# Eight tiles of u fetched at the first dense tile, later Gelus, and three rows moved from v to u, in a decoder trunk with expert retrieval

## The chip, the cores and the metric

The kernel runs on one core of one Trainium2 chip. The metric is the device time of one execution in microseconds (us), lower is better.

## The reference

Two pre-norm residual layers over 256 positions of width 1024. The first layer's mixer is block-sparse attention beside chunkwise retention, the second's a gated short convolution. Each layer ends in an expert mixer (PEER), which is what the change touches:

```python
def peer(xn, w_q, sub_keys, u, v):
    ...
    q = (t @ w_q).reshape(n_tok, PEER_HEADS, 2, PEER_DKEY // 2)
    sc = jnp.einsum('thpd,hpnd->thpn', q, sub_keys).astype(jnp.float32)
    s1, i1 = lax.top_k(sc[:, :, 0], PEER_TOPK)
    s2, i2 = lax.top_k(sc[:, :, 1], PEER_TOPK)
    ...
    top_s, pos = lax.top_k(cand, PEER_TOPK)
    eidx = jnp.take_along_axis(cidx, pos, axis=-1)
    gate = jax.nn.softmax(top_s, axis=-1).astype(xn.dtype)
    ...
        hid = jax.nn.gelu(jnp.einsum('td,thkd->thk', tc, u[ec]), approximate=False)
        return jnp.einsum('thk,thkd->td', gc * hid, v[ec])
```

Per token, 8 heads choose 16 of 16,384 experts each; the token's product with the chosen rows of u goes through a Gelu and a gate, and weighs the chosen rows of v.

## The kernel before

The 256 tokens of the expert mixer are split. For 96 of them (`TG`) the 128 chosen rows of u, and later of v, are fetched from memory one expert slot at a time: one indirect DMA of POOL's queue brings 128 rows of 1024 floats (a "row" below, 192 per layer: 96 of u, then 96 of v). For the other 160 (`TD`) all experts are computed densely: 128 tiles of u, each [128, 1024], are multiplied with the tokens, and Gelu and a gate matrix G, built from one-hot matrices, give HG; then 128 tiles of v are multiplied with HG.

So a layer's mixer has these stages:

- Query tiles: 16 tiles of `wq`, each split in a high and a low part (pools `hi` and `lo`, 3 buffers each), with the scores against the keys (`ko`) one tile behind. VectorE runs the top-16 searches from a list of pieces (`pump`).
- u: the loop over 128 dense tiles `dense_u(i)`. Each uses one of four PSUM tiles. ScalarE's Gelu (L1400, L1402) and, once G has begun, VectorE's product (L1403) read it. Up to about tile 54 VectorE still works off the pump; then the indices are turned (`idx_tr`), and from about tile 61 G is built, 40 groups, two per three tiles.
- v: the loop over 128 tiles of v, 95 of them split in two parts by ScalarE (L1378) and VectorE (L1385).

Dense tiles come through a ring of 8 raw buffers (`Stream`): a load on SP's queue is told when its buffer's tile eight before has been told to be used, and waits on the queue until TensorE is done with it. SP's queue is in order: whatever stands behind a waiting load waits too. 22 of the 128 u tiles (`PRE`, tile number to buffer number) don't go through the ring: `fetch(i)` loads them into memory that is idle at that time. Fourteen go into the area of HG and the accumulators of the rows and are fetched during the query tiles (`early`). The other eight go into buffers that come free only after the last query tile (`early_u`, in this order: tile 58 into a `lo` buffer and `one`, 64 and 76 into `hi` buffers, 82 into `Xb`, 94 into a `hi` buffer, 106 into two `lo` buffers, 23 and 43 into the keys' `ko`). They are told one per dense tile, i = 1 to 8, each behind that tile's ring load.

The rows run beside all that (`Gather`): six buffers; `consume` tells VectorE's work on the next row (L985 for u, L1002 for v) and `issue` tells POOL to fetch the next one into the buffer. `ga.rate` is the number of rows consumed per dense tile: 0.6 for the first 8, 0.9 in tiles 8 to 45, 0.6 until G begins, then what brings the count to `UPTO[l]` rows (112 in layer 0, 110 in layer 1) at tile 117; the rest of the 192 is spread over v. After each quarter of 32 rows of u, `later` holds two pieces that are told when a later row is consumed: ScalarE's Gelu of the sums of those 32 rows (L991), 2 rows after the quarter's last, and VectorE's product with the gates (L992), 4 rows after it.

Of the kernel before, what the change touches and what calls it, by code (L numbers as in the profile page):

```python
# [14 lines left out]
AF = mybir.ActivationFunctionType  # L15
OP = mybir.AluOpType
# [12 lines left out]
NK = 128  # L29
# [13 lines left out]
GT = 4  # L43
UNIT = 2.0 ** 15
SCR = 11 * D
UPTO = (112, 110)
SPL = [i for i in range(NK) if i % 2 or i % 4 == 0 and i > 0]
CODE = 64.0
WHOLE = 1.5 * 2.0 ** 23
# [3 lines left out]
CALM = 11  # L53
# [141 lines left out]
def trunk_kernel(ctx, tc, x, small, cst, mcst, ew_in, ew_out, ow_in, ow_out, wq, keys, pu, pv, pun, gains, out):  # L195
    nc = tc.nc
    v = nc.vector
    act = nc.scalar
# [51 lines left out]
    def nm(s):  # L250
        uid[0] += 1
        return f"{s}{uid[0]}"
# [414 lines left out]
    def new_ko(dtype=F32):  # L667

        n = NPAIR * NK * (2 if dtype is F16 else 1)
        xv["ko"] = pers.tile([P, n], dtype, tag="ko", name=nm("ko"))  # L670
        return xv["ko"]
# [266 lines left out]
    class Gather:  # L938
# [39 lines left out]
        def consume(self):  # L978
            s_ = self.c
            r = self.row(s_)  # L980
            j = s_ % STEPS
            q = j // SUB
            w = self.hid[:, j:j + 1]
            if s_ < STEPS:
                v.scalar_tensor_tensor(r, r, 1.0, XG[:, q % 2, :], op0=OP.mult, op1=OP.mult, accum_out=w)  # L985
                if s_ == SUB - 1:
                    gp.dma_start(XG[TG:, 0, :], XG[2 * SUB:TG, 0, :])
                if j % SUB == SUB - 1:
                    w = self.hid[:, q * SUB:(q + 1) * SUB]
                    g = IG[:, 1, q * SUB:(q + 1) * SUB]  # L990
                    self.later[s_ + 2] = lambda: act.activation(w, w, AF.Gelu)  # L991
                    self.later[s_ + 4] = lambda: v.tensor_tensor(w, w, g, OP.mult)  # L992
            elif j % SUB == 0:
                so_far = self.acc[q - 1] if q else h[:, 0, :]
                v.scalar_tensor_tensor(self.acc[q][:TG], r[:TG], w[:TG], so_far[:TG], op0=OP.mult, op1=OP.add)
                v.tensor_scalar(self.acc[q][TG:], r[TG:], w[TG:], None, op0=OP.mult)
                if q:
                    self.part(q - 1)
                if q == 2:
                    self.later[s_ + 8] = self.fold  # L1000
            else:
                v.scalar_tensor_tensor(self.acc[q], r, w, self.acc[q], op0=OP.mult, op1=OP.add)  # L1002
            self.later.pop(s_, lambda: None)()
            self.c += 1
# [17 lines left out]
    def peer(l, before, norm):  # L1022
        with tc.tile_pool(name=nm("hg"), bufs=1) as hp:
# [36 lines left out]
            ga = Gather(hp)  # L1060
# [8 lines left out]
            def fetch(i):  # L1069

                k = PRE[i]
                if k < 11:
                    t = [flat[:, k * D:(k + 1) * D]]
                elif k < 14:
                    t = [ga.acc[k - 11]]
                elif 14 < k < 18:
                    t = [st.hi_pool.tile([P, D], F32R, tag="hi", name=nm("uhi")).bitcast(F32)]
                elif k > 19:  # L1080
                    if k == 20:
                        there["ko"] = new_ko().rearrange("p (a d) -> p a d", a=2)
                    t = [there["ko"][:, k - 20, :]]
                elif k == 18:
                    t = [Xb.rearrange("p k s -> p (k s)").bitcast(F32)]
                else:
                    n = 1 if k == 14 else 2
                    t = [st.lo_pool.tile([P, D], BF16, tag="lo", name=nm("ulo")).bitcast(F32) for _ in range(n)]
                    t += [one] * (2 - n)
                n = D // len(t)  # L1090
                for j, p in enumerate(t):
                    nc.sync.dma_start(p, pu[l, i][:, j * n:(j + 1) * n])
                there[i] = [p[:, c:c + P] for p in t for c in range(0, n, P)]
# [3 lines left out]
            early_u = [i for i in sorted(PRE) if PRE[i] >= 14]  # L1097
            early_u = early_u[2:] + early_u[:2]
# [184 lines left out]
            def after_first():  # L1283

                scores(NPAIR - 1)
                pump.add((1.35, stage1(0, NPAIR - 1, NPAIR)))
                chain(0, 1)
                pump.add((0.3, lambda: gates(0)), (0.6, lambda: places(1)))
                pump.add(*[(2.7, stage1(1, f, f + 2)) for f in range(HH * 2, NPAIR, 2)])
                pump.add((0.0, lambda: gates_exp(0)))  # L1290
                chain(1, 0)
                pump.add((0.6, lambda: gates_norm(0)), (0.3, shares))
                chain(1, 1)
                pump.add((0.3, lambda: gates(1)), (3.0, None), (0.0, lambda: gates_exp(1)), (3.0, None),
                         (0.6, lambda: gates_norm(1)), (3.0, None), (3.0, None), (0.5, idx_tr), (3.0, None))
# [3 lines left out]
            def onehots(g):  # L1299

                oh = xv["gate"][:, :6 * GT * P].rearrange("p (n j t i) -> p n j t i", n=3, j=2, i=P)[:, g % 3]
                hi = xv["gate"][:, 6 * GT * P:].rearrange("p (n t i) -> p n t i", n=2, i=P)[:, g % 2]
                v.tensor_tensor(oh, iota[:, None, None, :].to_broadcast([P, 2, GT, P]),  # L1303
                                idxT[:, :2, g * GT:(g + 1) * GT][:, :, :, None].to_broadcast([P, 2, GT, P]),
                                OP.is_equal)
                ohs[g] = oh[:, 0], hi, oh[:, 1]
# [32 lines left out]
            gst = {"g": -1, "credit": 0.0, "rate": 0.0}  # L1339

            def slot(n):

                g = gst["g"]
                shared()
                if g < 0 or g >= NG:
                    return
                gst["credit"] += gst["rate"]
                if gst["credit"] < 1.0:
                    return
                gst["credit"] -= 1.0  # L1350
                ps = g_mm(g)
                if g + 3 < NG:
                    onehots(g + 3)
                if g + 2 < NG:
                    todo.append(g + 2)
                g_put(g, ps, n)
                gst["g"] = g + 1

            def dense_u(i):
                if i in PRE:  # L1360
                    w = there.pop(i)
                else:
                    t = st.next()
                    w = [t[:, k * P:(k + 1) * P] for k in range(ND)]
                ps = acc_tile(i % 4, nm("hid")) if i % 4 < 2 else hid_tile(nm("hid"))
                for k in range(ND):
                    pe.matmul(ps[:, :TD], w[k], XF[:, k, :], start=k == 0, stop=k == ND - 1)  # L1367
                    if k == ND // 2 - 1:
                        slot(i)
                return ps  # L1370
# [17 lines left out]
            for i in range(NK):  # L1388
                ps = dense_u(i)
                if i == 0:  # L1390
                    after_first()
                elif early_u:
                    fetch(early_u.pop(0))
                if i == NK - 1:
                    gst["rate"] = 1.0
                    while gst["g"] < NG:
                        slot(i)
                T = max(gst["g"], 0) * GT
                if T < TD:
                    act.activation(HG[:, i, T:], ps[:, T:TD], AF.Gelu)  # L1400
                if T > 0:
                    act.activation(ps[:, :T], ps[:, :T], AF.Gelu)  # L1402
                    v.tensor_tensor(HG[:, i, :T], ps[:, :T], HG[:, i, :T], OP.mult)  # L1403
                slot(i + 1)
                if gst["g"] < 0:
                    if i == first_late - 2:
                        pump.flush()
                    if pump.q:
                        pump.run(1.4)
                    else:  # L1410
                        gst["g"] = 0
                        gst["rate"] = NG / (2.0 * (NK - 10 - i))
                        gst["credit"] = -0.6
                        xv["gate"] = new_ko(F16)
                        for g in range(3):
                            onehots(g)
                        todo += [0, 1]
                        shared()
                        shared()
                ga.rate = (0.9 if 8 <= i < 46 else 0.6) if gst["g"] < 0 else (UPTO[l] - ga.c) / (NK - CALM - i) if i < NK - CALM else 0.6  # L1420
                if i < NK - QUIET:
                    ga.step()
                elif i in (NK - QUIET, NK - QUIET + 2):
                    weight_parts(i - NK + QUIET + 1)
# [41 lines left out]
            for i in range(NK):  # L1466
                j = i + AHEAD
# [22 lines left out]
                w = st.next()  # L1490
# [85 lines left out]
```

## Time and profile before

| | us |
|---|---|
| median of 3 runs | 1489.36 (1488.99 to 1492.16) |
| the profiled execution | 1490.58 |
| its span, first to last instruction | 1488.8 |
| u of layer 0, about | 182 to 490 |
| v of layer 0, about | 490 to 751 |
| u of layer 1, about | 907 to 1212 |
| v of layer 1, about | 1212 to 1472 |

Busy shares of the span: TensorE 97%, VectorE 84%, ScalarE 51%, GpSimd 50%; mean granted TensorE clock 0.997. The DMA engines moved 532.80 MB, 358 GB/s over the span.

In the views, PE is TensorE's matmul and PEld its weight load, DVE VectorE, ACT ScalarE, POOL GpSimd, SPq the queue on which SP issues DMAs. A line of the chain is start, duration, and what; of the timeline start, duration, engine, line and operation; of the waits who waited for whom, the total in us, how often, and the longest.

### The profile page before, as it was taken

The page shows a single profiled execution, that of the slowest core. Times are in us where ns is not written, and L with a number is a line of the kernel's source. Part 1 is how long each engine was busy: PE and PEld are TensorE (multiplying, and loading weights), DVE is VectorE, ACT ScalarE, POOL GpSimd, SP SyncE. Part 2 cuts the span into 40 slices and gives each one's busy share as a digit, 9 for nine tenths or more (in the row PEclk, how much of TensorE's full clock was granted, in tenths as well). Part 3 has the DMA queues.
Part 4 walks back from the last instruction along what each step waited for, and adds up shares of the span by engine and source line. Part 5 has one row for each costly group of instructions (what it writes and reads, how often), then busy time and mean ns, then how long its engine had stood idle before and what let it go on. Part 6 is the DMA issues. An engine that isn't in the chain of part 4 may idle for free.

```text
span 1488.8 us, 30108 instructions
## 1 busy us (share of the span) xinstructions
PE 1438.1 (97%) x11184; PEld 1334.8 (90%) x11184; DVE 1246.5 (84%) x2467; ACT 761.3 (51%) x1825; POOL 744.9 (50%) x513
## 2 busy tenths in 40 slices
PE   9999999999999999999989999999999999999997
PEld 5667999999999998889889799999999999988886
DVE  5637999879999788888876589996899978888888
ACT  6556511258875454445564463212888745454544
POOL 6754545546667243345335374453566643443532
PEclk9999999999999999999999999999999999999999
DMA  8545899999999999999966478999999999999995
GB/s 322 199 145 203 311 378 409 395 409 408 405 402 396 394 400 405 406 394 404 409 242 230 169 277 326 407 408 396 408 405 401 399 397 407 399 408 409 398 406 228
DMA packets 147618, 532.80 MB, mean 358 GB/s; under 512 B 16976, under 2 KB 17360, under 8 KB 147472
## 3 DMA queue, kind: packets, MB, share of 16 engines
q1 hardware_dynamic: 72288, 258.43, 44.9%
q0 software_dynamic: 56608, 204.81, 35.1%
q10 hardware_dynamic: 18576, 67.64, 11.5%
q8 instruction: 88, 1.44, 0.4%
q14 instruction: 58, 0.48, 0.1%
HBM read 528.40 MB, written 1.05 MB: 356 GB/s over the span
## 4 chain that ended last, share of the span: by engine, by line
PE 54%; issue 17%; POOL 11%; DMA 9%; DVE 7%; ACT 2%; POOLq 0%; DVEq 0%; ACTq 0%; SPq 0%
PE hid L1367 30%; POOL rows L975 7%; PE hid L261 5%; DMA raw<-pu 4%; DMA raw<-pv 3%; POOL grow L975 3%; PE hid L267 2%; PE G L1327 2%; DMA rows<-pv,ig 2%; PE ea L295 2%; PE vo L1501 2%; PE ea L294 2%; PE ea L293 2%; DVE gacc L1002 1%; PE vo L1497 1%
## 5 line engine op out<-in xcount | busy, mean ns | idle before, releaser
L1367 PE MATMUL hid<-xf,raw 128*128 128x160 f32 x3392 | 487.4, 301 | 7.3 <-DMA raw<-pu 4.6
L1367 PEld LDWEIGHTS hid<-xf,raw 128*128 128x128 f32 x3392 | 467.1, 191 | 10.5 <-issue 5.6
L1378 ACT CAST vhi<-raw 128x1024 fp32r<-128x1024 f32 x190 | 198.5, 1046 | 266.1 <-DMA raw<-pv 218.9
L975 POOL DMA_INDIRECT rows<-pv,ig x128 | 192.5, 1504 | 209.2 <-DVE gacc L1002 180.0
L1385 DVE TENSOR_TENSOR vlo<-raw,vhi 128x1024 bf16<-128x1024 f32 x190 | 231.9, 1223 | 77.4 <-ACT vhi L1378 69.1
L1501 PE MATMUL vo<-ko,vhi 128*128 128x320 f32 x1520 | 270.5, 320 | 24.5 <-DVE ko L1460 23.5
L1501 PEld LDWEIGHTS vo<-ko,vhi 128*128 128x128 f32 x1520 | 224.3, 188 | 33.8 <-DVE ko L1460 32.5
L975 POOL DMA_INDIRECT rows<-pun,ig x128 | 170.7, 1334 | 136.0 <-DVE rows L985 63.2
L151 POOL TENSOR_TENSOR lo<-raw,hi 128x1024 bf16<-128x1024 f32 x70 | 167.9, 2408 | 85.7 <-ACT hi L149 82.8
L985 DVE SCALAR_TENSOR_TENSOR rows<-rows,xg 128x1024 f32<-128x1024 f32 x128 | 155.5, 1220 | 22.5 <-DMA rows<-pun,ig 22.4
L1400 ACT ACTIVATE hg<-hid 128x160 f32<-128x160 f32 (+14 forms) x240 | 62.7, 265 | 199.1 <-PE hid L1367 199.0
L1002 DVE SCALAR_TENSOR_TENSOR gacc<-rows,ghid,gacc 128x1024 f32<-128x1024 f32 x124 | 158.8, 1281 | 4.7 <-DMA rows<-pv,ig 3.9
L975 POOL DMA_INDIRECT grow<-pv,ig x64 | 99.7, 1558 | 122.8 <-DVE gacc L1002 110.9
L1497 PE MATMUL vo<-hg,raw 128*128 128x160 f32 x1056 | 157.3, 302 | 1.0 <-DVE hg L1403 1.0
L1497 PEld LDWEIGHTS vo<-hg,raw 128*128 128x128 f32 x1056 | 145.5, 190 | 1.4 <-DVE hg L1403 1.4
L1503 PE MATMUL vo<-hb,vlo 128*128 128x160 bf16 x1520 | 138.1, 234 | 2.1 <-DVE vlo L1385 2.1
L1317 ACT ACTIVATE ko<-ko,idxT 128x128 f16<-128x128 f16 x320 | 101.8, 390 | 51.1 <-DVE ko L1303 50.9
L1503 PEld LDWEIGHTS <-vlo 128*128 128x128 bf16 x1520 | 100.5, 98 | 22.1 <-DVE vlo L1385 3.1
L975 POOL DMA_INDIRECT grow<-pun,ig x64 | 81.3, 1270 | 77.6 <-DVE grow L985 43.3
L149 ACT CAST hi<-raw 128x1024 fp32r<-128x1024 f32 x100 | 102.8, 1046 | 30.0 <-PE hid L261 18.5
L261 PE MATMUL hid<-x,hi 128*128 128x256 f32 x800 | 107.4, 287 | 0.2 <-DVE cg L912 0.2
L1320 ACT ACTIVATE ko<-ko,idxT 128x128 f16<-128x128 f16 x320 | 101.1, 388 | 0.0
(251 smaller groups left out, 2097.2 us busy)
## 6 DMA issues: line engine op xcount, KB each, us to landing
raw<-pu SPq DMA_DIRECT2D x212, 512.0 KB, 7.9
raw<-pv SPq DMA_DIRECT2D x128, 512.0 KB, 8.9
raw<-pv ACTq DMA_DIRECT2D x128, 512.0 KB, 8.0
raw<-wq SPq DMA_DIRECT2D x32, 512.0 KB, 3.9
raw<-ew_in SPq DMA_DIRECT2D x28, 512.0 KB, 4.5
raw<-ow_in SPq DMA_DIRECT2D x24, 512.0 KB, 5.3
hg<-pu SPq DMA_DIRECT2D x22, 512.0 KB, 5.1
raw<-ew_out SPq DMA_DIRECT2D x8, 512.0 KB, 3.1
```

Of the source, the lines that this page charges most:

```text
L149: self.nc.scalar.copy(hi, t)
L151: eng.tensor_tensor(lo, t, hi.bitcast(F32), OP.subtract)
L261: pe.matmul(ps[:, :S], hi[:, k * P:(k + 1) * P], A2[:, k, s_, :], start=k == 0 and s_ == 0, stop=False)
L975: gp.indirect_dma_start(self.row(s_), None, table, bass.IndirectOffsetOnAxis(IG[:, 0, s_ % STEPS:s_ % STEPS + 1].bitcast(U32), 0))
L985: v.scalar_tensor_tensor(r, r, 1.0, XG[:, q % 2, :], op0=OP.mult, op1=OP.mult, accum_out=w)
L1002: v.scalar_tensor_tensor(self.acc[q], r, w, self.acc[q], op0=OP.mult, op1=OP.add)
L1367: pe.matmul(ps[:, :TD], w[k], XF[:, k, :], start=k == 0, stop=k == ND - 1)
L1378: act.copy(whi[j], raw)
L1385: v.tensor_tensor(wlo[j], raw, whi[j].bitcast(F32), OP.subtract)
L1497: pe.matmul(vo[b][:, :TD], w[:, b * P:(b + 1) * P], HG[:, i, :], stop=False, **m)
L1501: pe.matmul(vo[b][:, :2 * TD], hi[:, b * P:(b + 1) * P], hs, stop=i == NK - 1, **m)
L1503: pe.matmul(vo[b][:, :TD], lo[:, b * P:(b + 1) * P], hb, stop=i == NK - 1, **m)
```

## The change

Three edits in the expert mixer, the same in both layers. The eight fetches of `early_u` are all told at i = 0, behind the last scores, instead of one each at i = 1 to 8. The Gelu of the fetched sums is told 12 rows after its quarter's last row instead of 2, and the product with the gates 16 rows after instead of 4. And three more rows are consumed in u: `UPTO` is (115, 113), with a rate of 0.93 instead of 0.9 in tiles 8 to 45; the rate over v is worked out from what is left, so v has three rows fewer.

```diff
-UPTO = (112, 110)
+UPTO = (115, 113)
...
-                    self.later[s_ + 2] = lambda: act.activation(w, w, AF.Gelu)
-                    self.later[s_ + 4] = lambda: v.tensor_tensor(w, w, g, OP.mult)
+                    self.later[s_ + 12] = lambda: act.activation(w, w, AF.Gelu)
+                    self.later[s_ + 16] = lambda: v.tensor_tensor(w, w, g, OP.mult)
...
                 if i == 0:
                     after_first()
-                elif early_u:
-                    fetch(early_u.pop(0))
+                    for j in early_u:
+                        fetch(j)
...
-                ga.rate = (0.9 if 8 <= i < 46 else 0.6) if gst["g"] < 0 else (UPTO[l] - ga.c) / (NK - CALM - i) if i < NK - CALM else 0.6
+                ga.rate = (0.93 if 8 <= i < 46 else 0.6) if gst["g"] < 0 else (UPTO[l] - ga.c) / (NK - CALM - i) if i < NK - CALM else 0.6
```

## The prediction

> **What bounds the kernel now.** I read the page's rates first, then the chain of waits around the start of the dense u tiles, the SP queue's timeline there, the same stretches by windows, and the waits.
>
> ```profile
> span 1488.8 us, 30108 instructions
> GB/s 322 199 145 203 311 378 409 395 409 408 405 402 396 394 400 405 406 394 404 409 242 230 169 277 326 407 408 396 408 405 401 399 397 407 399 408 409 398 406 228
> raw<-pu SPq DMA_DIRECT2D x212, 512.0 KB, 7.9
> ```
>
> A slice is 37.2 us. From the sixth to the twentieth slice (layer 0) and again from the twenty-sixth to the thirty-ninth (layer 1) the DMA engines stand at 378 to 409 GB/s and never rise above 409: a ceiling. Those are the two experts' mixers. By stage (PE, PEld, DVE, ACT, POOL busy, clock, DMA share, GB/s), with the last hole before each plateau first, then u, u, v, v:
>
> ```profile
> 182.00:190.00 8.00, 8.00 (x63) 8.00 (x61) 7.55 (x24) 3.75 (x9) 2.52 (x4) 1.00 0.46 172
> 907.00:918.00 11.00, 11.00 (x84) 11.00 (x83) 10.31 (x39) 4.06 (x10) 4.92 (x7) 1.00 0.60 216
> 190.00:490.00 300.00, 295.99 (x2329) 292.83 (x2328) 271.68 (x660) 153.84 (x561) 169.54 (x126) 0.99 1.02 404
> 918.00:1212.00 294.00, 290.68 (x2302) 287.53 (x2301) 266.16 (x642) 151.34 (x556) 162.12 (x121) 1.00 1.02 404
> 490.00:751.00 261.00, 247.38 (x2058) 232.54 (x2057) 222.43 (x204) 129.06 (x164) 106.47 (x72) 1.00 1.02 402
> 1212.00:1470.00 258.00, 245.04 (x2040) 230.65 (x2039) 221.92 (x204) 128.55 (x163) 108.78 (x75) 1.00 1.02 403
> ```
>
> So in u TensorE and the DMA engines are both full (296 of 300 us; 404 GB/s), and in v the DMA engines alone. A tile or a fetched row is 512 KB, 524,288 B / 404 GB/s = 1.30 us of all DMA engines: my price for everything moved. The v stage ends with rows on the chain, and ScalarE waits for raw tiles of v all through it:
>
> ```profile
> 736.49 14.85 DMA rows<-pv,ig
> 1462.03 9.59 DMA rows<-pv,ig
> ```
>
> ```profile
> ACT vhi L1378 <- DMA raw<-pv: 218.9, 102, 4.9
> ACT hg L1209 <- DVE hg L1205: 6.7, 2, 4.1
> ACT ghid L991 <- DVE grow L985: 6.2, 2, 3.8
> ```
>
> **The eight fetches.** Today one is issued per tile, each behind the raw load of its tile on SP's queue (layer 0, then layer 1):
>
> ```profile
> 178.84 0.56 SPq L1092 DMA_DIRECT2D one<-pu  x1
> 187.53 0.33 SPq L134 DMA_DIRECT2D raw<-pu  x1
> 187.90 0.43 SPq L1092 DMA_DIRECT2D uhi<-pu  x1
> ...
> 202.28 0.33 SPq L1092 DMA_DIRECT2D ko<-pu  x1
> ```
>
> ```profile
> 904.28 0.43 SPq L1092 DMA_DIRECT2D one<-pu  x1
> 912.23 0.33 SPq L134 DMA_DIRECT2D raw<-pu  x1
> ...
> 928.21 0.33 SPq L1092 DMA_DIRECT2D ko<-pu  x1
> ```
>
> The first (ulo and one) is out by 178.84. The raw at 187.53 waits until TensorE has done with tile 1, and the other seven stand behind it and its followers: SP idles 8.7 us (8.0 in layer 1) while the DMA engines drain. The buffers are free far sooner:
>
> ```profile
> 182.25 0.45 PE sc L1117 x4
> 182.70 2.18 PE hid L1367 x16
> 184.87 0.44 PE sc L1117 x4
> 185.32 19.56 PE hid L1367 x144
> 204.88 19.64 DMA raw<-pu
> 224.52 0.14 issue
> 224.65 84.50 PE hid L1367 x608
> ```
>
> The last query tile's matmuls, which read the last hi, lo and Xb, end at 182.25; the keys (ko) are read last by the four at 184.87, done at 185.3. With all eight told at i = 0 they are ahead of that raw on the queue, and SP (some 0.4 us an issue) has two uhi out near 179.5, xb, uhi and two ulo near 182.5 to 184, both ko by 186. Seven tiles are 9.1 us of DMA work. The hole is worth 8 x (1 - 172/404) = 4.6 us in layer 0 and 11 x (1 - 216/404) = 5.1 us in layer 1; I take 0.3 us off each, since xb and the two ko come free only inside the hole: **4.3 and 4.8 us** of DMA work done before the plateau. Bounds: 0 (SP held elsewhere) and the whole 4.6 and 5.1. Fetched rows come from POOL's queue and start after the hole; the raws behind the burst keep their issue time.
>
> What TensorE gets of it directly: 16 instructions are a tile, 19.56 / 9 = 2.17 us. The raw issued at 204.88 took 19.64 us to land, against a lead of seven other raw buffers, 7 x 2.17 = 15.2 us, 19.5 with two prefetched tiles between; TensorE waited:
>
> ```profile
> 204.88:224.65 19.77, 17.63 (x129) 17.20 (x128) 1.00 1.03 408
> 918.73:952.04 33.31, 30.89 (x224) 30.25 (x224) 1.00 1.03 409
> 225.25:228.67 3.42, 3.42 (x15) 3.42 (x14) 3.42 (x19) 0.00 (x0) 2.62 (x2) 0.50 1.02 407
> 946.00:950.00 4.00, 1.93 (x15) 1.72 (x14) 3.93 (x10) 0.30 (x1) 1.75 (x2) 1.00 1.03 410
> ```
>
> Eight tiles in 19.77 us are 2.4 us late, and the 38 after them (608 in 84.50) another 1.9, since the granted clock was 0.50 for 3.4 us behind the wait: 4.3 us. Layer 1: 14 tiles in 33.31 us, 2.9 us late. With 4.3 us less queued, a raw lands in at most 15.3 us and this wait should go. The Trainium skill, TensorE: Matmul & The Clock Gate, Part 1, has the clock halved after an idle window of about 3.4 us; layer 0's wait is about 2 us, so by it the clock would have held and only 2.4 us could come back there. The row at 0.50 disagrees; layer 1's similar wait, at 1.00, agrees. The measured 4.3 stands.
>
> **Three rows from v to u.** Rows per tile rise from 0.90 to 0.93 in tiles 8 to 45, 1.1 rows, and the other 1.9 go to the stretch with G. A row is 1.30 us of DMA, and on VectorE:
>
> ```profile
> L1002 DVE SCALAR_TENSOR_TENSOR gacc<-rows,ghid,gacc 128x1024 f32<-128x1024 f32 x124 | 158.8, 1281 | 4.7 <-DMA rows<-pv,ig 3.9
> L985 DVE SCALAR_TENSOR_TENSOR rows<-rows,xg 128x1024 f32<-128x1024 f32 x128 | 155.5, 1220 | 22.5 <-DMA rows<-pun,ig 22.4
> ```
>
> V is bound by DMA, so it is 3 x 1.30 = **3.9 us shorter** per layer. In u they cost between 0 (they find idle DMA) and 3.9 us of DMA plus a VectorE lateness. Parts of u in layer 0:
>
> ```profile
> 224.00:280.00 56.00, 55.35 (x395) 55.38 (x396) 55.62 (x219) 10.30 (x28) 31.31 (x26) 0.97 1.03 408
> 282.00:316.00 34.00, 34.00 (x253) 34.00 (x253) 22.04 (x41) 8.20 (x22) 13.42 (x14) 1.00 1.03 396
> 420.00:472.00 52.00, 50.13 (x417) 48.44 (x417) 51.89 (x77) 40.52 (x160) 36.67 (x23) 1.00 1.02 397
> ```
>
> There is little idle DMA, and VectorE has room only in the middle one (12 us), where it waits for rows. I take the full 3.9 us of DMA: u moves by -4.3 + 3.9 and -4.8 + 3.9, v by -3.9 each. What VectorE adds at the end of u (full, 51.89 of 52) overlaps with the late rows; I count nothing for it, up to 1.9 x 1.28 = 2.4 us a layer if it doesn't. Sum: -(4.3 + 4.8) = **-9.1 us**; the three rows only move time from v to u.
>
> **The Gelus.** Today ScalarE meets the Gelu of the sums two rows after the last of them, and waits 6.2 us in two places, with TensorE not idle: four hid tiles of 2.17 us are 8.7 us of cover. Told twelve rows later it waits for nothing, and the products stand before their first reader (row 96 needs the one of row 47; the last comes at row 111, within the 113 or 115 of u). Cost 0. Its worth shows when TensorE runs 4.3 us ahead of a VectorE that is full from 224 to 280: without it the longest wait would be 3.8 + 4.3 = 8.1 us, at the edge of the cover. What is late next is the other wait of this kind, L1209 behind L1205: at most 4.1 + 4.3 + 1.3 (a row) = 9.7, so up to 1.0 us of new idle per layer, which eats of the head start and not of the DMA time. After it come the waits at the end of u on VectorE's products (L1403).
>
> **The forecast.** The profiled execution took 1490.58 us, its span 1488.8, so 1.8 us lie around it; less 9.1 it is 1481.5. The median of the runs, 1489.36, lies 1.2 lower: 1480.2, say **1480**. A difference of 0.2% (3 us) is what can be told from no change.
>
> **Rivals.**
> - *The rows ride free.* If the raws' shorter backlog leaves DMA to the rows, TensorE's waits vanish from u (4.3 and 2.9) and v is still 3.9 shorter each: -15.0, 1474. For it: VectorE waits for rows 22.4 us at L985. Against: 404 of 409 GB/s. The Trainium skill, DMA: Bandwidth & Descriptors, Queues, rings and completion order, has each DMA engine go round-robin between the queues that have work, so a raw backlog would hold the rows to half; by it the rows gain most here. No row of this trace splits the rate by queue.
> - *The gain is lost on demand.* VectorE, full from 224 to 280, asks for rows no sooner, the DMA engines idle later for what they did earlier, and TensorE waits at the first G: 0, 1489. A half-lost gain is 1485. Against: the rate in 282 to 316, where VectorE already waits for rows.
> - *VectorE takes over, slower.* Three rows at 1.28 are 3.8 us a layer more in u, if its full stretches set u's end, and v, 247 us of TensorE in 261, is set by that chain and gives nothing back: +7.6, 1497. It decides if VectorE's idle time in u is under 3.8 us. Against: 12 us idle in 282 to 316, and the 218.9 us of waits for v tiles.
> - *The fetches start no earlier*, if SP is held by a buffer's release later than the matmuls above: rows alone, neutral, 1489.
>
> **Chances.** The forecast with losses up to half, 1476 to 1485: 0.62. Rows free, 1472 to 1476: 0.14. Gain lost or fetches no earlier, 1485 to 1492: 0.15, of it 0.09 within 0.2% and 0.06 below. Slower: 0.09. Faster by over 0.2% is 0.62 + 0.14 + 0.06 = 0.82, within it 0.09, slower 0.09. The range, 1473 to 1487, leaves out the slower case, most of the lost one and the tail below.
>
> **What would show it.** Right: seven fetches on SP before 187; over 380 GB/s in 182 to 190 and 907 to 918; no wait of TensorE for raw tiles of u; u ending 0 to 2 us earlier, v 3 to 5 us shorter in each layer; no wait at L991. Wrong: an issue gap on SP still there; u ending later than now; v not shorter; TensorE waiting at L1367 for L1403 by more than the 2.4 us allowed; GB/s under 400 over u.

## The result, and the profile after

The changed kernel takes 1486.2 us (median; 1481.68 to 1491.52) beside 1489.17 us (1487.96 to 1492.16) of the kernel before: ratio 0.9977, 95% interval 0.9968 to 0.9986. It is 3 us faster, where 9.1 us were forecast. The profiled execution took 1487.02 us. The span and the rates of its page:

```profile
span 1485.1 us, 30106 instructions
GB/s 323 199 146 202 329 409 406 396 393 397 408 408 406 405 397 409 406 393 407 408 248 214 148 317 387 409 401 392 405 406 408 394 401 397 408 409 395 384 383 198
```

The sixth slice, the start of layer 0's plateau, has risen from 378 to 409 GB/s: the hole is filled. New are the 384 and 383 near the end, where 398 and 406 stood.

The first 10 us of u (its first dense matmul starts at 182.5 us before and 182.4 after in layer 0, at 907.2 and 900.7 in layer 1) by windows, before and then after; columns as in the prediction:

```profile
182.20:192.20 10.00, 10.00 (x77) 10.00 (x76) 9.41 (x33) 4.06 (x10) 4.10 (x6) 1.00 0.57 207
906.90:916.90 10.00, 10.00 (x77) 10.00 (x76) 9.41 (x33) 4.06 (x10) 4.13 (x6) 1.00 0.55 201
```

```profile
182.20:192.20 10.00, 10.00 (x77) 10.00 (x77) 9.38 (x35) 4.01 (x10) 1.52 (x3) 1.00 1.02 391
900.70:910.70 10.00, 10.00 (x77) 10.00 (x76) 9.38 (x35) 3.82 (x10) 1.92 (x4) 1.00 1.03 400
```

That is 10 x (391 - 207)/404 = 4.6 us and 10 x (400 - 201)/404 = 4.9 us of DMA work done earlier. SP's timeline in the changed kernel:

```profile
179.16 1.00 SPq L1092 DMA_DIRECT2D uhi<-pu  x2
182.09 0.33 SPq L1092 DMA_DIRECT2D xb<-pu  x1
182.47 0.64 SPq L1092 DMA_DIRECT2D uhi<-pu  x1
183.17 1.48 SPq L1092 DMA_DIRECT2D ulo<-pu  x2
185.16 0.80 SPq L1092 DMA_DIRECT2D ko<-pu  x2
187.34 2.50 SPq L134 DMA_DIRECT2D raw<-pu  x2
```

All fetches are out before the raw of 187.34. What replaced the old waits stands in the groups and the waits of the changed kernel (waiter, releaser, us in total, times, longest):

```profile
L1367 PE MATMUL hid<-xf,raw 128*128 128x160 f32 x3392 | 483.5, 300 | 1.0 <-DVE hg L1403 0.8
L985 DVE SCALAR_TENSOR_TENSOR rows<-rows,xg 128x1024 f32<-128x1024 f32 x128 | 154.8, 1216 | 4.6 <-DMA rows<-pun,ig 3.2 <-issue 1.2
L1367 PE MATMUL hid<-xf,hg 128*128 128x160 f32 x352 | 53.3, 306 | 7.0 <-ACT hg L1400 7.0
```

```profile
ACT vhi L1378 <- DMA raw<-pv: 200.5, 95, 4.8
ACT hg L1209 <- DVE hg L1205: 17.2, 2, 8.8
```

TensorE's matmuls with raw tiles now idle 1.0 us in all, and none of it for a raw tile. But it idles 7.0 us behind ScalarE's Gelus (L1400), and ScalarE's wait at L1209, the exp of the second half of the gates, has grown from 6.7 to 17.2 us. In the group of L985 shown, VectorE's wait for rows has fallen from 22.4 to 3.2 us.

How the wait passes through ScalarE to TensorE, layer 0, in ScalarE's timeline before and after (start, duration, operation, idle before):

```profile
287.78 1.28 ACT L1209 ACT_TABLE_LOAD   x1
291.75 0.31 ACT L1209 ACTIVATE hg<-hg 128x128 f32<-128x128 f32 x1 [2.69 <-DVE hg L1205]
292.08 1.28 ACT L1400 ACT_TABLE_LOAD   x1
```

```profile
283.10 0.30 ACT L1400 ACTIVATE hg<-hid 128x160 f32<-128x160 f32 x1 [1.87 <-PE hid L1367]
283.42 1.28 ACT L1209 ACT_TABLE_LOAD   x1
293.11 0.31 ACT L1209 ACTIVATE hg<-hg 128x128 f32<-128x128 f32 x1 [8.41 <-DVE hg L1205]
293.44 1.28 ACT L1400 ACT_TABLE_LOAD   x1
294.74 0.89 ACT L1400 ACTIVATE hg<-hid 128x160 f32<-128x160 f32 x4
```

TensorE runs ahead, so ScalarE meets the exp 4.4 us earlier, and VectorE's input to it (L1205) comes 1.4 us later. ScalarE loads the exp's table, waits 8.41 us, does the exp and loads the Gelu's table again. No hid tile is freed between 283.4 and 295.0. The waits of TensorE at 295.1 (layer 0) and 1013.9 (layer 1), and the windows right behind them:

```profile
PE hid L1367 <- ACT hg L1400: 3.3, 1, 3.3
```

```profile
PE hid L1367 <- ACT hg L1400: 3.7, 1, 3.7
```

```profile
295.20:298.60 3.40, 3.40 (x13) 3.40 (x14) 2.35 (x5) 0.43 (x3) 2.79 (x3) 0.50 1.02 408
1013.90:1017.30 3.40, 3.38 (x25) 3.38 (x26) 2.25 (x5) 0.86 (x4) 2.79 (x3) 1.00 1.04 410
```

3.3 us of idle and 3.4 us at half clock in layer 0 (13 matmuls where layer 1 does 25), 3.7 us of idle in layer 1: that is the head start.

The second loss is in v of layer 1. POOL's timeline, then VectorE's, of the changed kernel there:

```profile
1395.25 0.94 POOL L975 DMA_INDIRECT rows<-pv,ig  x1 [1.79 <-DVE gacc L1002]
1398.61 18.00 POOL L975 DMA_INDIRECT grow<-pv,ig  x1 [2.42 <-DVE gacc L1002]
1416.91 0.94 POOL L975 DMA_INDIRECT grow<-pv,ig  x1 [0.30 <-issue]
```

```profile
1397.06 1.28 DVE L1002 SCALAR_TENSOR_TENSOR gacc<-grow,ghid,gacc 128x1024 f32<-128x1024 f32 x1
1398.37 1.22 DVE L1008 TENSOR_TENSOR gacc<-gacc,gacc 64x1024 f32<-64x1024 f32 x1
1399.51 1.21 DVE L1385 TENSOR_TENSOR vlo<-raw,vhi 128x1024 bf16<-128x1024 f32 x1
...
1413.44 2.35 DVE L1385 TENSOR_TENSOR vlo<-raw,vhi 128x1024 bf16<-128x1024 f32 x2
1422.12 1.28 DVE L1002 SCALAR_TENSOR_TENSOR gacc<-grow,ghid,gacc 128x1024 f32<-128x1024 f32 x1 [6.33 <-DMA grow<-pv,ig]
```

```profile
1396.00:1417.00 21.00, 20.76 (x174) 19.59 (x173) 19.76 (x19) 12.35 (x17) 18.28 (x3) 1.00 0.94 360
```

A gather mostly takes 0.9 to 2.0 us of POOL (97% of all in the profiles of this document), this one 18.00 (4.1 in the kernel before). It starts inside the fold (L1008, with which VectorE adds what is left of the first two sums to the third, told behind row 168) and ends 0.8 us after VectorE has run out of work at 1415.8. Meanwhile no row is fetched, the rate falls to 360 GB/s, and VectorE then waits 6.33 us for the next row.

VectorE is then late with L1460, the low part of HG that TensorE needs. TensorE's two longest waits in v of layer 1, and the windows behind them:

```profile
1425.16 2.50 PE L1501 MATMUL vo<-ko,vhi 128*128 128x320 f32 x8 [3.85 <-DVE ko L1460]
1460.05 2.50 PE L1501 MATMUL vo<-ko,vhi 128*128 128x320 f32 x8 [3.06 <-DVE ko L1460]
```

```profile
1425.00:1428.40 3.40, 3.24 (x15) 3.04 (x16) 3.40 (x4) 0.70 (x1) 2.03 (x2) 0.50 1.03 416
1459.10:1465.90 6.80, 5.86 (x26) 5.45 (x27) 6.76 (x8) 1.56 (x4) 0.00 (x0) 0.50 0.65 257
```

TensorE waits 3.85 and 3.06 us and works through 10.2 us at half clock. In the kernel before, its longest wait in this stage is 1.4 us and the clock stays at 1.00. (One more stretch at 0.50, from 1373.8 to 1377.2, lies ahead of the long gather and is not due to it.)

### The profile page after: what moved, and what is told of

Read it like the earlier page. It is cut to its first block, busy times and chain, and to the rows that moved or that the text cites. A ratio compares the mean times of both kernels' runs of the same rounds, so it can differ in the third digit from the quotient of the medians.

```text
span 1485.1 us, 30106 instructions
## 1 busy us (share of the span) xinstructions
PE 1436.9 (97%) x11184; PEld 1339.1 (90%) x11184; DVE 1244.8 (84%) x2467; ACT 763.2 (51%) x1825; POOL 748.9 (50%) x513
## 4 chain that ended last, share of the span: by engine, by line
PE 42%; DVE 22%; DMA 14%; issue 13%; POOL 7%; ACT 2%; POOLq 0%; SPq 0%; ACTq 0%; DVEq 0%
PE hid L1367 22%; DMA raw<-pv 9%; POOL rows L975 5%; DVE rows L985 3%; PE hid L261 3%; POOL grow L975 3%; PE G L1327 2%; PE vo L1501 2%; DVE grow L985 2%; PE ea L295 2%; PE ea L294 2%; PE ea L293 2%; DVE hg L1106 2%; DVE hg L1112 2%; DMA rows<-pv,ig 2%
## 5 line engine op out<-in xcount | busy, mean ns | idle before, releaser
L1367 PE MATMUL hid<-xf,raw 128*128 128x160 f32 x3392 | 483.5, 300 | 1.0 <-DVE hg L1403 0.8
L1367 PEld LDWEIGHTS hid<-xf,raw 128*128 128x128 f32 x3392 | 465.2, 190 | 2.1 <-DVE hg L1403 1.3
L1378 ACT CAST vhi<-raw 128x1024 fp32r<-128x1024 f32 x190 | 198.5, 1046 | 264.0 <-DMA raw<-pv 200.5
L975 POOL DMA_INDIRECT rows<-pv,ig x128 | 181.8, 1420 | 229.9 <-DVE gacc L1002 197.7
L1501 PE MATMUL vo<-ko,vhi 128*128 128x320 f32 x1520 | 274.8, 323 | 23.1 <-DVE ko L1460 22.8
L1385 DVE TENSOR_TENSOR vlo<-raw,vhi 128x1024 bf16<-128x1024 f32 x190 | 231.4, 1222 | 77.0 <-ACT vhi L1378 54.5
L1501 PEld LDWEIGHTS vo<-ko,vhi 128*128 128x128 f32 x1520 | 228.5, 191 | 28.9 <-DVE ko L1460 28.3
L1400 ACT ACTIVATE hg<-hid 128x160 f32<-128x160 f32 (+14 forms) x240 | 62.4, 265 | 220.2 <-PE hid L1367 191.6
L975 POOL DMA_INDIRECT grow<-pv,ig x64 | 113.6, 1775 | 106.0 <-DVE gacc L1002 92.0
L985 DVE SCALAR_TENSOR_TENSOR rows<-rows,xg 128x1024 f32<-128x1024 f32 x128 | 154.8, 1216 | 4.6 <-DMA rows<-pun,ig 3.2
L1497 PE MATMUL vo<-hg,raw 128*128 128x160 f32 x1056 | 157.3, 302 | 1.2 <-DVE hg L1403 1.1
L1497 PEld LDWEIGHTS vo<-hg,raw 128*128 128x128 f32 x1056 | 145.5, 190 | 1.7 <-DVE hg L1403 1.7
```

Source lines behind the costliest of these rows:

```text
L975: gp.indirect_dma_start(self.row(s_), None, table, bass.IndirectOffsetOnAxis(IG[:, 0, s_ % STEPS:s_ % STEPS + 1].bitcast(U32), 0))
L1378: act.copy(whi[j], raw)
L1385: v.tensor_tensor(wlo[j], raw, whi[j].bitcast(F32), OP.subtract)
L1497: pe.matmul(vo[b][:, :TD], w[:, b * P:(b + 1) * P], HG[:, i, :], stop=False, **m)
L1501: pe.matmul(vo[b][:, :2 * TD], hi[:, b * P:(b + 1) * P], hs, stop=i == NK - 1, **m)
```

## The experiments

The theories: A, the wait at L1209 gives TensorE's head start back; B, DMA sets the end of u whatever TensorE does; C, the loss is POOL's long gather in v. All stages from one profiled execution each: u from the first matmul of L1367 to the first of L1497, v from there to the layer's closing matmuls. Two executions of the changed kernel differ by up to 3.1 us in one stage (268.2 and 265.1), so a difference of under 3 us in a single stage shows little by itself. The profiles of gelu_early and after_fold are of executions 4.0 and 3.3 us under their kernels' medians, that of fold_stt is of one 5.6 us above. The wait is the one before the exp of L1209, in layers 0 and 1; the gather is the one behind the fold in layer 1. The kernels ran in four groups: after_again, exp_later, no_rows and rows_only; burst_later, gelu_early, fold_later and part_later; before_later, rows_short, fold_last and rows_less; after_fold and fold_stt. The kernel before, beside each group, had medians of 1489.55 to 1490.42; across groups the ratios compare better than the medians.

| kernel | median us | ratio to before, 95% | u0 | v0 | u1 | v1 | wait | gather |
|---|---|---|---|---|---|---|---|---|
| before | 1489.17 | | 306.9 | 263.3 | 304.6 | 264.5 | 2.7, 4.1 | 4.1 |
| changed | 1486.2 | 0.9968 to 0.9986 | 306.6 | 257.3 | 303.6 | 268.2 | 8.4, 8.8 | 18.0 |
| after_again | 1486.49 | 0.9967 to 0.9989 | 305.9 | 258.4 | 305.2 | 265.1 | 8.1, 8.9 | 18.0 |
| exp_later | 1482.49 | 0.9940 to 0.9973 | 306.1 | 258.6 | 303.8 | 262.5 | 1.4, 2.9 | 8.2 |
| no_rows | 1486.12 | 0.9953 to 0.9979 | 303.4 | 264.9 | 302.2 | 264.0 | 7.1, 7.6 | 4.1 |
| rows_only | 1493.29 | 1.0012 to 1.0030 | 311.4 | 257.7 | 308.5 | 262.7 | 6.6, 5.1 | 6.5 |
| burst_later | 1479.47 | 0.9919 to 0.9946 | 301.9 | 261.5 | 299.4 | 264.8 | 1.4, 1.2 | 4.1 |
| gelu_early | 1485.12 | 0.9956 to 0.9981 | 305.7 | 257.1 | 303.6 | 262.1 | 7.3, 7.3 | 8.2 |
| fold_later | 1481.31 | 0.9931 to 0.9958 | 305.8 | 257.2 | 304.3 | 261.8 | 1.6, 3.2 | 4.1 |
| part_later | 1480.98 | 0.9929 to 0.9956 | 306.8 | 256.9 | 303.3 | 261.3 | 1.7, 1.9 | 4.1 |
| before_later | 1489.48 | 0.9988 to 1.0010 | 306.9 | 261.7 | 303.8 | 264.2 | 0, 0 | 4.1 |
| rows_short | 1483.28 | 0.9932 to 0.9958 | 304.3 | 257.4 | 303.1 | 268.5 | 1.3, 2.1 | 18.0 |
| fold_last | 1482.92 | 0.9936 to 0.9962 | 300.7 | 262.0 | 300.1 | 266.8 | 0.1, 0 | none |
| rows_less | 1489.32 | 0.9990 to 1.0007 | 299.9 | 270.9 | 299.8 | 268.1 | 0, 0 | under 3.3 |
| after_fold | 1483.11 | 0.9938 to 0.9970 | 306.2 | 257.1 | 302.3 | 261.8 | 8.2, 7.5 | none |
| fold_stt | 1485.99 | 0.9959 to 0.9983 | 307.1 | 259.2 | 304.6 | 268.6 | 8.2, 8.2 | 16.9 |

The granted clock in v goes with its length: the six profiles with a stretch at 0.50 in v of layer 1 (changed, after_again, rows_short, fold_last, rows_less, fold_stt) are the six longest there, 265.1 to 268.6 us; the other ten take 261.3 to 264.8. In v of layer 0 the two with such a stretch (no_rows, rows_less) are the two longest, 264.9 and 270.9. All four profiles with a gather of 16.9 or 18.0 us in layer 1 are among the six. No run takes the halved clock away by itself.

**after_again**: the changed kernel once more.

> The changed kernel once more, for a second profile. Theory A (the wait of ScalarE at the exp of the gates, L1209, for VectorE's extraction gives the head start of TensorE back): again a wait at L1209 of 8 us or more in each layer, TensorE idle 3 to 4 us behind it, u 301 to 305 us long; the stage v of layer 1 is 258 to 262 us long if the 18 us in one gather of POOL at 1398 were an accident of that execution. Rival C (the loss is in v: POOL stops for long in every execution of the changed kernel): a gather of 10 us or more again in v, and v of layer 1 270 us long. Time 1486 +- 4 by both.

Measured 1486.49 us: the wait and the 18.0 us gather are there again, at the same places, so neither was an accident. v of layer 1, 265.1 us, lies between the two theories' figures; u, 305.9 and 305.2, a little above theory A's.

**exp_later**: the list of VectorE's pieces holds idle places; one is moved ahead of the exp, one taken from behind its norm.

```diff
-pump.add((0.3, lambda: gates(1)), (3.0, None), (0.0, lambda: gates_exp(1)), (3.0, None),
-         (0.6, lambda: gates_norm(1)), (3.0, None), (3.0, None), (0.5, idx_tr), (3.0, None))
+pump.add((0.3, lambda: gates(1)), (3.0, None), (3.0, None), (0.0, lambda: gates_exp(1)), (3.0, None),
+         (0.6, lambda: gates_norm(1)), (3.0, None), (0.5, idx_tr), (3.0, None))
```

(Several expectations below call this edit "the norm told later". It moves the exp one idle place later, and the norm behind it with it.)

> The changed kernel with the exp of layer's last gates told one pad (about two tiles, 4.3 us) later on ScalarE. Theory A: the wait at L1209 falls from 8.4 to about 4 us, inside the 8.7 us that four hid tiles cover, TensorE has no idle time there, u ends 4 to 5 us (layer 0, with the halved clock) and 3 to 4 us (layer 1) earlier, and the time falls by 5 to 8 us against the changed kernel, to about 1479. Rival B (DMA sets the end of u whatever TensorE does): the same time moves to waits of TensorE for VectorE's products at L1403 at the end of u or into v, and the time stays within 2 us of 1486.

1482.49 us: 4.0 less than after_again beside it by the medians, 3.3 by the ratios, whose intervals overlap a little. That lies between the two theories' times. The wait is 1.4 and 2.9 us and TensorE has no gap of over 1.0 us left in u. Yet u is as long as before the edit; most of the difference lies in v of layer 1, where the gather fell to 8.2 us and the clock stays at 1.00. With the three rows in u, B holds for u. How the edit in u shortens a gather in v is not shown.

**no_rows** and **rows_only**: the change without the three rows, and the three rows alone.

```diff
 no_rows: changed kernel
-UPTO = (115, 113)
+UPTO = (112, 110)
-ga.rate = (0.93 if 8 <= i < 46
+ga.rate = (0.9 if 8 <= i < 46
 rows_only: kernel before, the same two lines the other way
```

> The changed kernel without the three rows (UPTO 112 and 110, rate 0.90): the burst of fetches and the late Gelus alone. The prediction's sum (9.1 us of DMA work done earlier, the rows neutral): 1480. Theory A: the wait at L1209 is there with one row less in front of it, about 7.5 us, TensorE idle some 2 us, u 1 to 2 us shorter than with the rows, v 3.9 us longer a layer: 1487 to 1491. Rival B: the rows are neutral, 1486.

> The kernel before with the three rows alone (UPTO 115 and 113, rate 0.93). The prediction's sum: neutral, 1489 +- 2. Theory A: the wait at L1209 grows to 4 to 5 us, still covered; v 3.9 us shorter a layer; u longer by 0 to 3.9 us as the raw tiles at its start come later: 1482 to 1489. Rival B: 1489.

Burst and Gelus alone: 1486.12, u 3.5 and 2.4 us shorter. Rows alone: 1493.29, u 4.5 and 3.9 us longer, v 5.6 and 1.8 us shorter. The rows pay in u what was forecast. In v of layer 0 they give it all back, in layer 1 1.8 us, which the spread of a single stage does not tell from 3.9. no_rows is 6 us above the prediction's sum, just under theory A's range and at B's figure; rows_only is slower than either theory and the sum allowed.

**burst_later**: no_rows and exp_later together. **before_later**: the kernel before with exp_later's edit alone.

> The changed kernel with the three rows back in v (UPTO 112 and 110, rate 0.9 again) and with the norm of the gates' exp told one pad later, so that ScalarE does not wait at L1209. Asks whether that wait costs time once the rows no longer load u. With the rows in v and the wait in place the two u took 303.4 and 302.2 us, with the wait at 7.1 and 7.6 us. Theory A (ScalarE's wait gives TensorE's head start back, about 2 us of idle and 1.7 us of halved clock in layer 0, 2.5 in layer 1): u at 300.0 to 301.5 and 299.7 to 300.5, median 1480 to 1483. Theory B (DMA's work sets the end of u, TensorE's stop is absorbed): u within 1 us of 303.4 and 302.2, median 1485 to 1487.

> The kernel before with only the norm of the gates' exp told one pad later. Asks what that edit is worth without the burst of fetches: there the waits at L1209 are 2.7 and 4.1 us, under the 8.7 us of hid tiles that TensorE has ahead. Theory A (the wait costs only what passes TensorE's cover, so the burst made it dear): 1488 to 1490, no difference. Rival J (telling the norm later is worth 4 to 6 us by itself, whatever the burst does): 1483 to 1486, and the burst of fetches is then worth only 4 to 6 us of the 10 between the kernel before and the one with the burst, the old rows and the norm later (1479.5).

burst_later takes 1479.47 us, just under theory A's range and the fastest here, 7.0 us under the changed kernel and 10 under the one before; before_later is at no difference. So with the old rows the wait costs 1486.12 - 1479.47 = 6.6 us by the medians, 5.1 by the ratios (theory A), and only because the burst made it long: where TensorE has no head start, telling the exp later is worth nothing. u by windows in burst_later:

```profile
182.00:484.00 302.00, 300.60 (x2382) 298.10 (x2381) 279.30 (x681) 157.24 (x567) 170.71 (x129) 1.00 1.02 404
900.00:1200.00 300.00, 300.00 (x2385) 298.48 (x2384) 277.30 (x679) 157.10 (x566) 161.99 (x127) 1.00 1.02 404
```

TensorE is busy 300.6 of 302 and 300.0 of 300 us. This u has no room left on TensorE: A holds where the old rows are kept.

**gelu_early**: the changed kernel with the Gelus at their old places (2 and 4 rows behind a quarter).

> The changed kernel with the Gelus told two and four rows after the last sum again, as before the change. Asks what that part of the change is worth. The prediction's reading: with TensorE ahead of a full VectorE the longest wait at L991 is about 8 us against 8.7 us of cover in four hid tiles, so 0 to 1 us per layer, median 1486 to 1488. Rival: ScalarE stops at L991 behind VectorE in each layer for more than its cover, as it does at L1209, TensorE idles 2 to 4 us at one or two places per layer and the clock is halved behind them: median 1489 to 1494.

1485.12 us, under both forecasts and no slower than the changed kernel (1486.49). Its waits:

```profile
ACT ghid L991 <- DVE grow L985: 17.6, 2, 9.3
ACT hg L1209 <- DVE hg L1205: 14.6, 2, 7.3
```

The wait at L991 comes, 8.3 and 9.3 us, and stops TensorE by 0.44 and 1.42 us. The wait at L1209, shorter for that, stops it by 2.25 us in each layer.

**rows_short**: exp_later with three sums of u's last rows cut short.

```diff
+            elif s_ in (100, 104, 108):
+                v.scalar_tensor_tensor(self.acc[q][:, :32], r[:, :32], w, self.acc[q][:, :32], op0=OP.mult, op1=OP.add)
```

> The changed kernel with the norm later, in which VectorE adds rows 100, 104 and 108 of each layer only in 32 of their 1024 elements (their gathers stay whole; the output lacks the rest). Asks which work of the three rows in u has the price of 4.2 and 4.4 us (306.1 and 303.8 us of u with them, 301.9 and 299.4 without): three gathers of 512 KB are about 3.8 us of DMA time, three sums of 1.27 us are 3.8 us of VectorE. Theory D (DMA): u stays at 305.5 to 306.5 and 303 to 304.5. Theory V (VectorE): u at 302 to 303 and 299.5 to 300.5, the median at 1477 to 1479.

u at 304.3 and 303.1 us: 1.8 and 0.7 less than exp_later, where the whole price of the rows is 4.2 and 4.4. Some 3.7 us of VectorE's work is gone in each layer, so the price leans to the DMA's side: layer 1 lies in D's band, layer 0 between the two. Differences of this size in one stage do not settle it. The 18.0 us gather is back, and v of layer 1 with it at 268.5.

**rows_less**: burst_later with UPTO (109, 107) and a rate of 0.87.

> The burst with the norm later and three rows fewer in u than before (109 and 107, rate 0.87), the other direction of the change. If a row costs in u what it costs above (1.4 us) down to there and gives 0.9 back in v: u 4 us shorter, v 3 us longer in each layer, median 1477 to 1478. If u is bound by TensorE's own matmuls there: u at most 1 us shorter, v 3 to 4 us longer, median 1483 to 1486.

1489.32 us, worse than either case: u 2.0 us shorter and 0.4 longer, v 9.4 and 3.3 us longer. u stays at the 300 us that TensorE is busy in burst_later. In v of layer 0 POOL's and VectorE's timelines and TensorE's longest wait are:

```profile
681.37 16.87 POOL L975 DMA_INDIRECT grow<-pv,ig  x1 [3.46 <-DVE gacc L1002]
```

```profile
696.21 1.21 DVE L1385 TENSOR_TENSOR vlo<-raw,vhi 128x1024 bf16<-128x1024 f32 x1
705.74 1.29 DVE L1002 SCALAR_TENSOR_TENSOR gacc<-grow,ghid,gacc 128x1024 f32<-128x1024 f32 x1 [8.32 <-DMA grow<-pv,ig]
```

```profile
PE vo L1503 <- DVE vlo L1385: 9.1, 4, 6.9
```

The same stall, now in layer 0, at the same row: 16.87 us of POOL, then 8.32 us of VectorE and up to 6.9 us of TensorE.

**fold_later**, **part_later**, **fold_last**, **after_fold**, **fold_stt**: where and how the fold is told. The first two start from exp_later, fold_last from burst_later, the others from the changed kernel.

```diff
-self.later[s_ + 8] = self.fold
+self.later[s_ + 20] = self.fold    # fold_later, part_later
+self.later[s_ + 28] = self.fold    # fold_last, after_fold
 part_later also: the DMA of the second partial sum
-self.part(q - 1)
+self.later[s_ + 6] = lambda: self.part(1)
 fold_stt
-v.tensor_tensor(a[2][:2 * SUB], a[0][:2 * SUB], a[2][:2 * SUB], OP.add)
+v.scalar_tensor_tensor(a[2][:2 * SUB], a[0][:2 * SUB], 1.0, a[2][:2 * SUB], op0=OP.mult, op1=OP.add)
```

> The kernel with the exp's norm told later, and with the fold of the third sum (VectorE adds two of its quarters) told at row 180 instead of row 168 of each layer's 192. Asks what the long gather of row 174 of layer 1 hangs on (18.0 us in the changed kernel, 8.2 with the norm later, 4.1 in the kernel before). Theory F (it is the first gather told behind the fold that stalls): the long one moves to about row 186 and row 174 takes 1 to 2 us; the median stays at 1481 to 1483. Rival G (place in GpSimd's program or in time, nothing to do with the fold): row 174 stays at 4 to 18 us.

> The kernel with the exp's norm later and the fold at row 180, and the DMA of the second partial sum (L1012, on GpSimd's queue) told at row 166 instead of row 160. Same question for that DMA: Theory H (the long gather is the one that stands a fixed number of rows behind that DMA, 14 rows now): it moves by six rows, to about row 180 of layer 1. Rival G (place in the program or in time): row 174 stays long at 4 to 18 us. If it shrinks to 1 to 2 us without another one growing, v of layer 1 falls from 262.5 to about 259 us and the median to 1478 to 1480.

> The burst with the old rows and the norm later, and the fold told at row 188 of each layer, where no gather is left to be told behind it. Theory F (the long gather is the first one behind the fold): no gather of over 4 us is left in v (now 5.8 at row 174 of layer 0 and 4.1 in layer 1), v at 260 to 261.5 and 262.5 to 264.5, median 1477 to 1479.5. Rival G (place in the program): a gather of over 4 us stays.

> The changed kernel, its wait at L1209 left in place, with the fold told at row 188, where no gather is told behind it. Asks what the gather of 18.0 us in layer 1 costs by itself. Theory C' (the gather that starts inside the fold cannot write its descriptors until VectorE has a gap between two instructions; with three rows more in u VectorE has none for 17 us there, and v of layer 1 pays 3 to 5 us): no gather over 4 us in v, v of layer 1 at 261 to 264 us (265.1 and 268.2 in two executions of the changed kernel), median 1482 to 1484.5. Rival B' (DMA catches up behind the stall, only the wait at L1209 costs): v of layer 1 at 265 or more without the stall, median 1486 to 1487.

> The changed kernel with the fold in another form at the same place: the scalar_tensor_tensor that VectorE uses for the rows, with the factor 1.0, in place of tensor_tensor. Asks whether the long gather hangs on the form of the instruction in which it starts or on the place. By form: no gather over 4 us at row 174, v of layer 1 at 261 to 264 us, median 1482 to 1484.5. By place (any two-input instruction that starts behind a wait of VectorE holds the gather off until VectorE's next gap): the gather of row 174 of layer 1 takes about 18 us again, ending 0.8 us after the first boundary of two VectorE instructions that do not follow without a gap; median 1486 to 1487.

With the fold told 12 rows later the long gather of layer 1 moves by 12 rows (row 186, 4.1 us), and one of 5.8 us appears at row 186 of layer 0, where exp_later had none of over 3.4, wherever the partial sum's DMA is told. That is theory F; G and H fall. With no gather behind the fold, there is none of over 3.4 us in v. The other form of the instruction changes nothing: POOL's timeline of fold_stt, row 174 of layer 1:

```profile
1401.39 16.86 POOL L975 DMA_INDIRECT grow<-pv,ig  x1 [2.96 <-DVE gacc L1002]
```

So it is the place, not which of these two forms. The price: after_fold, which has TensorE's stop at L1209 still (3.2 us at most), takes 1483.11 us, 3.4 less than after_again (3.6 by the ratios) and 2.9 less than fold_stt beside it (2.5 by the ratios); its interval overlaps with both of theirs. v of layer 1 is at 261.8, as C' expected; the four profiles with 17 to 18 us there have 265.1 to 268.6. But fold_last, which takes away gathers of 5.8 and 4.1 us, is 3.4 us slower than burst_later (2.5 by the ratios, with overlapping intervals), where 0 to 2.5 us of gain were expected, with v of layer 1 at 266.8. There VectorE has the fold ahead of the last piece of L1385; TensorE waits 1.93 us for that piece, up to 1461.7, and runs at 0.50 from 1461.9 to 1465.3. So the long stall costs 2.5 to 3.6 us by these figures, the short one is not shown to cost anything, and whether a fold at row 188 costs time in every execution of fold_last is not settled.

## Why the prediction was right and wrong

By stages the sum said -0.4 and -0.9 us for u of the two layers and -3.9 us for each v. The two profiles of the changed kernel have -0.3 and -1.0, then -1.0 and +0.6, for u; -6.0 and -4.9 for v of layer 0; +3.7 and +0.6 for v of layer 1. So u came out as forecast within the spread of a stage, and the term of the sum that failed is v of layer 1. The prediction also mis-sized the cover of a wait in u; with the old rows that alone takes half of the gain (no_rows beside burst_later), with the new ones it does not lengthen u.

- **The eight fetches: right.** 4.6 and 4.9 us of DMA work moved into the hole (forecast 4.3 and 4.8), fetches out before 187.3, no wait for raw tiles. Without the wait that follows, burst_later shows u 5.0 and 5.2 us shorter. Its 1479.47 us is the forecast 1480, from another kernel than the one forecast.
- **"What is late next": the cover was mis-sized.** The prediction named the wait at L1209, put it at 9.7 us at most and compared it with 8.7 us of cover. The wait was 8.4 and 8.8 us, inside that bound. But it was covered for 5.07 us, not 8.7: TensorE idles 8.41 - 3.34 = 5.07 us less than ScalarE waits in layer 0, 8.77 - 3.70 = 5.07 in layer 1, 7.33 - 2.25 = 5.08 in gelu_early. The four hid tiles must also cover what ScalarE does around the exp: 1.28 + 0.31 + 1.28 us of table loads and exp and the next Gelu's 0.30, 3.2 us, and some 0.5 us more. The loads and the exp stood in the trace of before (287.78 to 292.08). With them a 9.7 us wait would have been forecast at 9.7 + 3.2 - 8.7 = 4.2 us of idle per layer instead of 1.0. The halved clock, seen before behind layer 0's wait, was not put on the new one.
- **"Of the head start and not of the DMA time": wrong with the old rows, right for u with the new ones.** With the old rows TensorE sets u (300.0 of 300 us in burst_later), and the wait costs 5.1 to 6.6 us. With three more rows u is no longer with the wait than without it (306.6 and 303.6 beside 306.1 and 303.8).
- **The three rows: "V is bound by DMA, so it is 3.9 us shorter" is the term that failed, in layer 1.** Their price in u was right: 4.5 and 3.9 us alone, forecast 3.9. The gain in v held in layer 0 (5.6 alone; 6.0 and 4.9 in the changed kernel) and failed in layer 1: 3.7 and 0.6 us longer in two executions of the changed kernel. v has a term that the sum lacked, POOL's gather behind the fold, which grew from 4.1 to 18.0 us; the trace of before held it at 4.13 us. Behind it TensorE waits for VectorE and its clock is halved. With the stall gone v of layer 1 is 2.7 us shorter than in the kernel before (after_fold). With wait and long stall both gone it is 2.7 and 3.2 us shorter (fold_later, part_later), and these kernels take 8.2 and 8.5 us less than before by the ratios, most of the 9.1 forecast. The rows then cost 1481.31 - 1479.47 = 1.8 us instead of nothing, which the intervals of the two kernels do not tell from nothing.
- **The Gelu edit at 0: right**, to what can be told (1485.12 with the old places, 1486.49 with the new ones). The wait forecast without it, 8.1 us "at the edge of the cover", was 8.3 and 9.3 us and let TensorE idle 0.44 and 1.42 us. No table is loaded there, and the cover was 7.9 us. What this stop takes, the wait at L1209 gives back, 1.1 and 1.5 us shorter than in the changed kernel.
- **The rivals.** "The rows ride free" fell: full price in u. "The fetches start no earlier" fell with the SP rows. "VectorE takes over" gave the sign of rows_only, 3 to 4 us slower; whether its cause holds there is not settled, though rows_short leans to the DMA. "A half-lost gain", 1485, is the nearest to what came; its place was given as VectorE's demand for rows, and it was ScalarE's wait and POOL's stall.

So of the 6 us between forecast and result, by the medians taking away the wait at L1209 gives 4.0 back (exp_later, most of it in v of layer 1, through the shorter gather) and taking away the stall 3.4 (after_fold); both, 5.2 to 5.5 (fold_later, part_later). They overlap and do not add up. Both together are clear of the changed kernel's interval; either alone overlaps with it a little.

## What to carry to other kernels

When an engine is given a head start, list every wait of the engines that feed its buffers, and compare the cover with the whole block between two releases, table loads included, not with the wait alone. A head start is worth only what the tightest such block lets through; the block was free as long as TensorE was late itself, so the two edits (earlier fetches, exp told later) are worth 10 us together, and 3 to 5 and 0 alone. Work moved from one stage to another is paid back only if the receiving stage's other chains, here POOL's, are as short as its bound.

## What the runs showed of the hardware

A gather that starts inside the fold is held until VectorE has a gap. Over the 16 profiles each gather of over 4 us (20 cases, 4.1 to 18.0 us) starts 0.23 or 0.24 us into the fold and ends 0.81 to 0.82 us after a boundary of two VectorE instructions with a gap. At all boundaries before it in the gather, VectorE's next instruction starts 72 ns or more ahead of the recorded end of the last; at this one 44 ns ahead at most, mostly 35 ns to 8 us behind it. After 1413.44 + 2.35 = 1415.79 VectorE is empty, and the gather ends at 1416.61. In the eight other cases of a gather that starts inside the fold, the gap comes at once: VectorE's next instruction starts 35 or 36 ns behind the fold's end, and the gather is through 0.81 or 0.82 us later, after 1.8 us. Where VectorE is behind its work there may be no gap until it runs out of fetched rows, which the gather itself holds back; that is how 4 us become 18. The Trainium skill, SBUF — State Buffer, Who interferes with whom, says that a VectorE instruction with two inputs from SBUF and a GpSimd instruction that reads SBUF exclude each other through a shared port, the second blocked until the first finishes. The runs agree in that the gather is held by VectorE's work; they differ on the length, since up to 16 instructions of VectorE end before the gather goes on. That a port is what holds it no run here shows. Why other gathers, which also start under such instructions, mostly pass at the end of the first, in 0.9 to 2.0 us, is open.

The clock: behind 3.34 us of idle in layer 0 the granted clock was 0.50 for 3.4 us, behind 3.70 us in layer 1 it was 1.00. The length of the wait alone does not decide it; what goes with it is how much of the wait falls into one step of a grid. In every trace the stretches at 0.50 start on a grid of 3413.3 ns, to within 2 ns. Over the 16 traces TensorE was busy for less than 0.45 of the step in 41 of the 43 steps at full clock that such a stretch followed (0.54 and 0.55 in the other two), and for 0.47 or more in all but 4 of the 6847 that none followed (0.43 and 0.44 there). The 3.34 us fell into one step (busy 0.03 of it), the 3.70 us on two (0.48 and 0.44). So the two waits of the kernel before part as well: 1.90 us in one step (0.44) was followed by 0.50, 2.07 us on two (0.57 and 0.78) was not.
